# Attention constants dealt out again, rotary finishing steps at other key tiles, first transfers in another order, in a one-core encoder layer on Trainium2

## The chip, the cores and the metric

One core of a Trainium2 chip runs the whole layer. The metric is the device time of one execution in microseconds (us). The engines are TensorE (PE, with its weight loads PEld), VectorE (DVE), ScalarE (ACT), GpSimd (POOL) and SyncE (SP, which issues most transfers).

## What is computed

A hybrid encoder layer on x of 1024 positions by 1024, all in float32:

```
h = rms_norm(x, norm1_g);  z = h @ w_in            # 1024 x 2304: qA kA vA qB kB vB
A: q, k = rope(rms_norm(q)), rope(rms_norm(k))     # 8 q heads, 2 kv heads, 2-D axial rotary
   o_A = softmax(q k^T / 8) v                      # dense, over all 1024 keys
B: three dilated windows with ALiBi, merged by their softmax denominators
x1 = x + concat(norm(o_A), norm(o_B)) @ w_out
y  = x1 + (gelu(gate) * val) @ w_down              # gate, val: conv of rms_norm(x1) @ w_up
```

## The kernel before

The program is written as one Python function that emits instructions; a scheduler sets the final order on each engine, so the order shown below is that of the compiled program. PE runs every large product in three passes of high and low parts (lines such as L279 to L281 and L405 to L407), and the input, up and down projections as seven products in place of eight.

**Start, 0 to 57 us.** SP loads the identity (`ident`, L518), the first tile of x in halves (L520), `norm1_g` (L521), then in turn two halves of the k and v columns of w_in (`kv_load`, L264) and further tiles of x. `x_prep` transposes a tile of x on PE (L180) and splits it into a high part by ACT (L228) and a low part by DVE (L229). `kv_split` does the same for the weights, scaled by norm1_g (L268 on ACT, L269 on DVE). `kv_proj(i)` multiplies tile i by those weights (L279 to L281), `x_rest` squares the tile for its norm (L244) and copies the transposed banks (L248), and `kv_out` evacuates the product (L291).

**Input projection, 27 to 208 us.** `in_product` makes 28 products; ACT evacuates them (L420 to L428) and DVE combines them (L417). The next weights are combined by DVE (L378 to L384) and split (L388 ACT, L389 DVE). Beside it keys and queries get their rotary steps: POOL's `turn` (L285, eight instructions), DVE's `norm` (L490), `cos` (L500), `add` (L503). `k_ready` transposes the keys and writes them to `R_K2A` and `R_KHA` (L332, L333). The unused partitions of `R_KHA` are filled with -1 by `fill_k` (L348), other constants by `fill` (L214).

**Attention A, about 211 to 430 us.** Sixteen blocks g of eight key tiles. A key tile is two products of scores (L624, L625), an exp on ACT (L627) and eight products with v (L619). Beside it the next block is prepared: `mx` makes eight products (L597), each with a maximum by DVE (L598) out of one of two banks, and `last` combines them (L601), to be transposed and evacuated (L605). L576 and L577 split the queries, L592 evacuates their transposes, L639 and L640 finish the output of the block before (`o_norm`). Two lists of further work are taken up beside it: `late`, the squares, root (L486, whose Sqrt needs ACT's table changed and changed back) and norms (L490, followed by POOL's L506) of the qB columns; and `fills`, nine constants for attention B. `late_plan` says how many items of `late` follow each key tile.

Attention B, the mixer and both projections of the MLP take the rest, to 1342 us.

```
act(f(slots[kt], 512), bank(st), AF.Exp)
take(prep, plan[kt])
take(late, late_plan[kt])
```

Of the kernel before, what the change touches and what calls it, by code (L numbers as in the profile page):

```python
# [14 lines left out]
AF = mybir.ActivationFunctionType  # L15
OP = mybir.AluOpType
# [3 lines left out]
D = 1024  # L20
# [12 lines left out]
O_IDF = 0  # L33
# [5 lines left out]
O_QAB = 832  # L39
# [5 lines left out]
R_KHA = R_K2A + 2048  # L45
# [12 lines left out]
R_A = {1: 0, 7: 4096, 6: 8192, 4: 12288, 5: 16384, 2: 20480, 3: 24576}  # L58
# [6 lines left out]
F_JNK = O_F + 4096  # L65
F_CST = O_F + 4608
F_KVT = O_F + 5120
F_KSQ = O_F + 4096
F_ROPE = O_F + 8192
# [3 lines left out]
R_QLN = R_XT + 1024  # L73
# [4 lines left out]
R_VB = R_XT + 8192  # L78
R_QLB = (R_XT + 1024, R_XT + 10240)
R_KN = R_XT + 12288  # L80
R_SET = (R_W, R_K2A)
# [42 lines left out]
def tile_encoder_layer(ctx, tc, x, w_in, gains, outg, norm1_g, norm2_g, w_out, w_up, conv_w, conv_b,  # L124
                       w_down, ident, rope, tmx, tbc, cnt, out):
    nc = tc.nc
# [12 lines left out]
    act = nc.scalar.activation  # L139
# [5 lines left out]
    def f(off, n):  # L145
        return bigf[:, off:off + n]

    def r(off, n):
        return bigr[:, off:off + n]

    def rf(off, n):
        return bigr[:, off:off + n].bitcast(F32)
# [8 lines left out]
    def rp(off, *dims):  # L161
        return raw_ap(bigr[:, off:off + 1], dims)
# [19 lines left out]
    def perm_rows(t, b, width):  # L182
        rr, c = divmod(b, 2)
        return bass.AP(tensor=t.tensor, offset=t.offset + (512 * c + rr) * width, ap=[[4 * width, 128], [1, width]])
# [24 lines left out]
    def qab(tt):  # L209
        return O_QAB + 1024 * tt  # L210

    def fill(dst, n, m, c):

        vec.tensor_scalar(dst, f(O_IDF, m)[:, None, :].to_broadcast([128, n, m]), 0.0, c, op0=OP.mult, op1=OP.add)  # L214

# [127 lines left out]

    def fill_k():
        for i in range(4):
            vec.tensor_scalar(r(R_KHA + 512 * i, 512)[64:128], f(F_ROPE, 512)[64:128], 0.0, -1.0,  # L348
                              op0=OP.mult, op1=OP.add)


    def w_buf(c, half):
# [162 lines left out]
            return [square, root, norm, k_out]  # L515
        return [square] + [root] * (late == 3), [norm, gain]

    dma(f(O_IDF, 128), ident)  # L518
    for i in range(2):
        dma(f(qab(0) + 512 * i, 512), perm_rows(x, 0, D)[:, 512 * i:512 * i + 512])  # L520
    dma(f(F_CST, 128)[0:8], norm1_g.rearrange("(k p) -> k p", p=128))  # L521
    for half in range(2):
        kv_load(half)
        dma(f(qab(1 + half), 1024), perm_rows(x, 1 + half, D))
    dma(f(qab(3), 1024), perm_rows(x, 3, D))
    w_load(0, 0)
    vec.tensor_copy(r(R_IDR, 128), f(O_IDF, 128))
    nc.tensor.transpose(bank(7, 8), f(F_CST, 128)[0:8], f(O_IDF, 8)[0:8])
# [51 lines left out]
    def a_prep(g):  # L580
        b, kv = divmod(g, 2)
        q2 = R_Q2A + 512 * (g % 2)
        ql = R_QLA + 512 * (g % 2)

        def nat():
            q_nat(qab(b) + 256 * kv, 64, vec, 4, 512 * kv)

        def first():
            t = next_tr()
            for i in range(4):  # L590
                tr_r(t, i, r(R_QD + 128 * (4 * kv + i), 128))
            act(r(q2, 512), bank(t), AF.Copy)  # L592

        def mx(i):
            for hf in range(2):
                b = hf
                mm(bank(b), r(q2 + 128 * i, 128), r(R_K2A + 1024 * kv + 512 * hf, 512), start=True, stop=True)  # L597
                vec.tensor_reduce(f(SM_MC + 8 * hf + i, 1), bank(b), axis=AX.X, op=OP.max)  # L598

        def last():  # L600
            vec.tensor_tensor(rp(R_QLN + 512 * kv + 64, [128, 4]), f(SM_MC, 4), f(SM_MC + 8, 4), op=OP.max)  # L601
            t = next_tr()
            for i in range(4):
                tr_r(t, i, r(R_QLN + 128 * (4 * kv + i), 128))
            act(r(ql, 512), bank(t), AF.Copy)  # L605

        return [nat, first] + [lambda i=i: mx(i) for i in range(4)] + [last]
# [309 lines left out]
        eng.tensor_tensor(r(o + 512, 512), t_raw(n, i), rf(o, 512), op=OP.subtract)  # L917


    fills = []  # L920
    for c, v in ((64, 1.0), (192, 0.0)):
        for i in range(2):
            fills.append(lambda o=R_VB + 1024 * i + c, v=v: fill(rp(o, [256, 4], [1, 64]), 4, 64, v))
    fills.append(lambda: fill(rp(R_QLB[1] + 64, [128, 8], [1, 64]), 8, 64, 0.0))
    for i in range(4):
        fills.append(lambda o=R_SET[0] + 2048 + 512 * i: vec.tensor_scalar(
            r(o, 512)[64:128], f(O_QAB, 512)[64:128], 0.0, -1.0, op0=OP.mult, op1=OP.add))

    def take(prep, n):
        for _ in range(n):  # L930
            if prep:
                p = prep.pop(0)
                if p:
                    p()

    prep = [lambda: fill(rp(R_QLN + 64, [128, 8], [1, 64]), 8, 64, 0.0)] + a_prep(0)
    for i in range(4):
        kv_proj(i)
        x_rest(i)
# [97 lines left out]
    for g in range(16):  # L1037
        prep = a_prep(g + 1) if g < 15 else [lambda: b_split(0)] + b_prep(0)
        tail = a_main(g, prep, tail, late, (3, 2, 2, 2, 2, 2, 2, 1) if g == 15 else (1, 1, 1, 1, 1, 1, 1, 0),
                      (0, 1, 1, 0, 1, 0, 1, 0) if g < 3 else (0, 0, 1, 0, 1, 0, 1, 0) if g < 7 else (0, 1, 0, 0, 0, 1, 0, 0))  # L1040
        if g == 7:
            dma(f(F_CNT, 384), cnt)
            gp.memset(fp(F_VCN + 64, [66, 8]), 1.0)
            load_vc(0)
        if g == 11:
            load_k(0)
            load_k(1)
        if g == 5:
            v_split(R_VB, F_VBN)
            load_v(1)  # L1050
        take(fills, 1)
    for t in tail:
        t()
    take(prep, 99)
# [401 lines left out]
```

## Time and profile before

| what | value |
|---|---|
| time, median of 3 runs | 1342.73 us (1342.39 to 1345.34) |
| the profiled execution | 1343.92 us, of which the span is 1342.2 us |
| PE busy | 1311.1 us, 98% of the span |
| DVE, ACT, POOL busy | 991.7 us (74%), 674.0 us (50%), 363.4 us (27%) |

The profiled execution is 1.19 us over the median and has 1.7 us around its span. With PE at 98%, the time is that of PE's work plus the stretches in which PE stands still.

### The profile page before, as it was taken

Reading aid. Unit: us, or ns where it says so; the run is one execution under the profiler, and the core shown is the slowest. Engines: PE = TensorE matmul, PEld = TensorE weight load, DVE = VectorE, ACT = ScalarE, POOL = GpSimd, SP = SyncE. Lnnn points to the kernel's source line nnn. Section 1 sums busy time; section 2 is a strip of 40 time slices with the busy share of each in tenths; the row PEclk is TensorE's granted clock in tenths of the full one; section 3 lists DMA queues with packets and bytes.
Section 4 is the critical chain, followed back from the end, with each engine's and each line's share of the span. In section 5 each row is a group of like instructions: output and inputs, shape, how many; then the busy total and the mean of one; then the engine's idle time right before and its main releaser. Section 6 shows DMA issues by size and latency. Waiting matters only on the chain.

```text
span 1342.2 us, 20068 instructions
## 1 busy us (share of the span) xinstructions
PE 1311.1 (98%) x7559; PEld 1134.9 (85%) x7559; DVE 991.7 (74%) x1613; ACT 674.0 (50%) x1057; POOL 363.4 (27%) x274
## 2 busy tenths in 40 slices
PE   8999999999999999999999999999999999999998
PEld 7999989989998888878877788888888888888887
DVE  4987696864545888876579877887787789586664
ACT  7855553644445776764365444444444445244331
POOL 1611123020001222100114565556656651100000
PEclk9999999999999999999999999999999999999999
DMA  7144212000001333252222233232233325897873
GB/s 256 53 123 114 80 39 65 9 9 0 1 1 34 107 105 81 67 166 79 94 87 71 102 110 111 86 102 96 102 115 105 102 101 190 283 311 228 293 223 113
DMA packets 119859, 148.08 MB, mean 110 GB/s; under 512 B 50833, under 2 KB 76881, under 8 KB 119761
## 3 DMA queue, kind: packets, MB, share of 16 engines
q1 hardware_dynamic: 118609, 143.65, 33.3%
q0 software_dynamic: 1152, 3.15, 0.9%
q8 instruction: 59, 0.97, 0.3%
q14 instruction: 39, 0.32, 0.1%
HBM read 112.95 MB, written 33.82 MB: 109 GB/s over the span
## 4 chain that ended last, share of the span: by engine, by line
PE 70%; DVE 16%; ACT 5%; issue 4%; POOL 4%; DMA 1%; SPq 0%; DVEq 0%; ACTq 0%; POOLq 0%
PE ps L619 7%; PE ps L1161 7%; PE ps L1162 7%; PE ps L1163 7%; PE ps L1277 5%; PE ps L1276 5%; PE ps L1278 5%; DVE bigf L1194 4%; PE ps L624 2%; PE ps L597 2%; PE ps L625 2%; POOL bigf L1208 2%; PE ps L862 2%; PE ps L795 2%; PE ps L864 2%
## 5 line engine op out<-in xcount | busy, mean ns | idle before, releaser
L1161 PE MATMUL ps<-bigr 128*128 128x512 f32 x616 | 241.1, 392 | 6.6 <-DVE bigf L1165 6.1
L1162 PE MATMUL ps<-bigr 128*128 128x512 f32 x616 | 239.8, 389 | 0.0
L1163 PE MATMUL ps<-bigr 128*128 128x512 f32 x616 | 239.7, 389 | 0.0
L1144 ACT ACTIVATE bigr<-bigf 128x512 fp32r<-128x512 f32 x154 | 92.8, 624 | 159.2 <-POOL bigf L1136 95.4
L1194 DVE SCALAR_TENSOR_TENSOR bigf<-bigf 128x768 f32<-128x768 f32 (+1 forms) x176 | 146.4, 889 | 26.3 <-ACT bigf L1192 26.3
L619 PEld LDWEIGHTS ps<-bigf 128*128 128x128 f32 x1024 | 139.4, 191 | 10.5
L1161 PEld LDWEIGHTS ps<-bigr 128*128 128x128 f32 x616 | 115.6, 188 | 35.6 <-DVE bigf L1165 9.9
L1145 DVE TENSOR_TENSOR bigr<-bigf,bigr 128x512 fp32r<-128x512 f32 x112 | 116.5, 1057 | 32.6 <-ACT bigr L1144 32.6
L1256 ACT ACTIVATE bigr<-bigf 128x1024 fp32r<-128x1024 f32 x77 | 80.6, 1059 | 119.5 <-PE ps L1278 76.9
L1163 PEld LDWEIGHTS ps<-bigr 128*128 128x128 f32 x616 | 115.6, 188 | 24.2
L1162 PEld LDWEIGHTS ps<-bigr 128*128 128x128 f32 x616 | 115.6, 188 | 23.6
L619 PE MATMUL ps<-bigf 128*128 128x65 f32 x1024 | 134.3, 267 | 0.0
L405 PE MATMUL ps<-bigr 128*128 128x256 f32 x448 | 127.2, 284 | 1.2 <-ACT bigf L291 1.2
L406 PE MATMUL ps<-bigr 128*128 128x256 f32 x448 | 126.8, 283 | 0.0
L407 PE MATMUL ps<-bigr 128*128 128x256 f32 x448 | 126.7, 283 | 0.0
L627 ACT ACTIVATE bigf<-ps 128x512 f32<-128x512 f32 x128 | 75.7, 597 | 93.5 <-PE ps L625 91.1
L1277 PE MATMUL ps<-bigr 128*128 128x512 f32 x308 | 119.9, 389 | 0.0
L1278 PE MATMUL ps<-bigr 128*128 128x512 f32 x308 | 119.8, 389 | 0.0
L1276 PE MATMUL ps<-bigr 128*128 128x512 f32 x308 | 119.8, 389 | 0.0
L1257 DVE TENSOR_TENSOR bigr<-bigf,bigr 128x1024 fp32r<-128x1024 f32 x77 | 93.0, 1221 | 28.7 <-ACT bigr L1256 26.7
L598 DVE TENSOR_REDUCE bigf<-ps 128x1 f32<-128x512 f32 x128 | 86.0, 689 | 23.6 <-PE ps L597 22.2
L1208 POOL TENSOR_TENSOR bigf<-bigf 128x512 f32<-128x512 f32 x44 | 69.1, 1590 | 89.9 <-DVE bigf L1199 65.6
(221 smaller groups left out, 2892.6 us busy)
## 6 DMA issues: line engine op xcount, KB each, us to landing
bigf<-w_down SPq DMA_DIRECT2D x99, 256.0 KB, 4.3
bigf<-w_up SPq DMA_DIRECT2D x44, 512.0 KB, 4.2
bigf<-gscr SPq DMA_DIRECT2D x77, 256.0 KB, 4.1
gscr<-bigf SPq DMA_DIRECT2D x33, 512.0 KB, 2.7
bigf<-w_in SPq DMA_DIRECT2D x8, 1024.0 KB, 5.3
bigf<-x SPq DMA_DIRECT2D x15, 512.0 KB, 6.6
bigf<-tmx SPq DMA_DIRECT2D x8, 672.0 KB, 5.1
bigf<-w_out SPq DMA_DIRECT2D x8, 512.0 KB, 4.0
```

What stands on the lines that cost most here:

```text
L405: mm(o, ah, wh, start=(k == 0 and t % 2 == 0 and n != 2), stop=False, skip_group_check=True)
L406: mm(o, ah, wl, start=False, stop=False, skip_group_check=True)
L407: mm(o, al, wh, start=False, stop=(k == 3), skip_group_check=True)
L619: mm(bank(ob, 65, 66 * i), f(slots[kt] + 128 * i, 128), f(F_VA + 132 * kt + 66 * kv, 65), start=(kt == 0 and i == 0), stop=(kt == 7), skip ...
L1145: (gp if n in (2, 4) and m > 3 else vec).tensor_tensor(rp(o + 512, [128, 4], [1, 128]), src, rfp(o, [128, 4], [1, 128]), op=OP.subtract)
L1161: mm(bank(b), wh, th, start=(k == 0 and n in (1, 5, 6, 7)), stop=False, skip_group_check=True)
L1162: mm(bank(b), wh, tl, start=False, stop=False, skip_group_check=True)
L1163: mm(bank(b), wl, th, start=False, stop=(k == 3), skip_group_check=True)
L1194: vec.scalar_tensor_tensor(f(a + o, n), f(i + d, n), w_, f(a + o, n), op0=OP.mult, op1=OP.add)
L1276: mm(o, ah, r(d, 512), start=(q == 0 and n in (1, 5, 2)), stop=False, skip_group_check=True)
L1277: mm(o, ah, r(d + 1024, 512), start=False, stop=False, skip_group_check=True)
L1278: mm(o, al, r(d, 512), start=False, stop=(q == NQ - 1), skip_group_check=True)
```

## The change

- `ident` and `norm1_g` are fetched by ACT's queue, ahead of its other work. SP's queue starts with the halves of x's first tile, then both halves of the k and v weights, and only then the other tiles of x.
- A one-element copy on DVE, out of the split weights into the scratch that `x_rest` writes its squares to, is put ahead of the loop over tiles.
- `fill_k` and the fill of `R_QLN` go from DVE to ACT.
- The nine `fills` are taken in blocks 4 to 12, one each, and read the output of the block before.
- `late_plan` has other numbers.

```
...
-    dma(f(O_IDF, 128), ident)
+    nc.scalar.dma_start(f(O_IDF, 128), ident)
+    nc.scalar.dma_start(f(F_CST, 128)[0:8], norm1_g.rearrange("(k p) -> k p", p=128))
     for i in range(2):
         dma(f(qab(0) + 512 * i, 512), perm_rows(x, 0, D)[:, 512 * i:512 * i + 512])
-    dma(f(F_CST, 128)[0:8], norm1_g.rearrange("(k p) -> k p", p=128))
     for half in range(2):
         kv_load(half)
-        dma(f(qab(1 + half), 1024), perm_rows(x, 1 + half, D))
-    dma(f(qab(3), 1024), perm_rows(x, 3, D))
+    for i in range(1, 4):
+        dma(f(qab(i), 1024), perm_rows(x, i, D))
...
-    def fill(dst, n, m, c):
+    def fill(dst, n, m, c, src=O_IDF, eng=None):
+        src = f(src, m)[:, None, :].to_broadcast([128, n, m])
+        if eng is None:
+            vec.tensor_scalar(dst, src, 0.0, c, op0=OP.mult, op1=OP.add)
+        else:
+            act(dst, src, AF.Copy, scale=0.0, bias=c)
...
-            vec.tensor_scalar(r(R_KHA + 512 * i, 512)[64:128], f(F_ROPE, 512)[64:128], 0.0, -1.0,
+            act(r(R_KHA + 512 * i, 512)[64:128], f(F_ROPE, 512)[64:128], AF.Copy, scale=0.0, bias=-1.0)
...
+    vec.tensor_copy(f(F_JNK, 1), rf(R_A[7] + 256, 1))
     for i in range(4):
         kv_proj(i)
         x_rest(i)
...
-                      (0, 1, 1, 0, 1, 0, 1, 0) if g < 3 else (0, 0, 1, 0, 1, 0, 1, 0) if g < 7 else (0, 1, 0, 0, 0, 1, 0, 0))
+                      (1, 1, 0, 0, 0, 0, 1, 1) if g < 3 else (0, 1, 0, 0, 0, 0, 1, 1) if g < 7 else (0, 1, 0, 0, 0, 0, 1, 0))
...
-        take(fills, 1)
+        if g > 3 and fills:
+            fills.pop(0)(qab((g - 1) // 2) + 256 * ((g - 1) % 2))
```

In the order of the compiled program the lines of the changed kernel have other numbers: L228 is L232 there, L244 L248, L248 L252, L268 L272, L291 L295; behind L340 three to seven are added (L382 is L385, L389 L392, L490 L493, L500 L503, L503 L506, L577 L580, L598 L601, L601 L604, L639 L642, L640 L643).

The first place is the start on ACT. Before, from its first row on:

```order
L228 ACT_TABLE_LOAD
L228 ACTIVATE bigr<-ps 128x512 x2
L268 ACTIVATE bigr<-bigf 128x256 x4
L244 ACTIVATE bigf<-bigf 128x1024
L228 ACTIVATE bigr<-ps 128x512
L268 ACTIVATE bigr<-bigf 128x256 x4
L228 ACTIVATE bigr<-ps 128x512
L248 ACTIVATE bigf<-ps 128x512 x2
L291 ACTIVATE bigf<-ps 128x256
```

The same place on ACT in the changed kernel:

```order
L521 DMA bigf<-ident 128x128
L522 DMA bigf<-norm_g 8x128
L232 ACT_TABLE_LOAD
L232 ACTIVATE bigr<-ps 128x512 x2
L272 ACTIVATE bigr<-bigf 128x256 x8
L232 ACTIVATE bigr<-ps 128x512 x2
L295 ACTIVATE bigf<-ps 128x256
L248 ACTIVATE bigf<-bigf 128x1024
L252 ACTIVATE bigf<-ps 128x512 x2
```

The eight weight splits now stand together, and the square and the two copies of tile 0 stand behind the first evacuation of a k and v product instead of ahead of it. On PE the 24 products of `kv_proj(0)` now stand without products of `kv_proj(1)` between them (before, six stood there), and with the eight transposes of x's second tile, as before.

The second place is DVE in the last products of the input projection, ahead of attention. Before:

```order
L490 TENSOR_TENSOR bigf<-bigf 128x4x256
L192 TENSOR_TENSOR bigf<-bigf 128x16
L214 TENSOR_SCALAR bigr<-bigf 128x8x64
L193 SCALAR_TENSOR_TENSOR bigf<-bigf 128x16
L348 TENSOR_SCALAR bigr<-bigf 64x512
L194 SCALAR_TENSOR_TENSOR bigf<-bigf 128x16
L348 TENSOR_SCALAR bigr<-bigf 64x512
L490 TENSOR_TENSOR bigf<-bigf 128x4x256
L348 TENSOR_SCALAR bigr<-bigf 64x512 x2
L382 TENSOR_TENSOR bigf<-bigf 128x4x256
L500 TENSOR_TENSOR bigf<-bigf 128x4x256
L577 TENSOR_TENSOR bigr<-bigf,bigr 128x4x64
```

The same place on DVE in the changed kernel:

```order
L493 TENSOR_TENSOR bigf<-bigf 128x4x256
L192 TENSOR_TENSOR bigf<-bigf 128x16
L385 TENSOR_TENSOR bigf<-bigf 128x4x256
L193 SCALAR_TENSOR_TENSOR bigf<-bigf 128x16
L503 TENSOR_TENSOR bigf<-bigf 128x4x256
L194 SCALAR_TENSOR_TENSOR bigf<-bigf 128x16
L392 TENSOR_TENSOR bigr<-bigf,bigr 128x1024
L493 TENSOR_TENSOR bigf<-bigf 128x4x256
L506 TENSOR_TENSOR bigf<-bigf 128x4x256
L580 TENSOR_TENSOR bigr<-bigf,bigr 128x4x64
```

The five fills are gone to ACT, and the weight sum (L382 before) now stands right behind L192, which is also what POOL's `turn` waits for; `cos` (L500 before) follows it, and a norm (L490) comes behind the split L389.

The third place is block 3 of attention A and the head of block 4, on DVE. Before:

```order
L191 RECIPROCAL bigf<-bigf 128x64
L598 TENSOR_REDUCE bigf<-ps 128x1 x3
L192 TENSOR_TENSOR bigf<-bigf 128x64
L598 TENSOR_REDUCE bigf<-ps 128x1
L193 SCALAR_TENSOR_TENSOR bigf<-bigf 128x64
L601 TENSOR_TENSOR bigr<-bigf 128x4
L194 SCALAR_TENSOR_TENSOR bigf<-bigf 128x64
L490 TENSOR_TENSOR bigf<-bigf 128x4x256
L577 TENSOR_TENSOR bigr<-bigf,bigr 128x4x64
L490 TENSOR_TENSOR bigf<-bigf 128x4x256 x2
L639 RECIPROCAL bigf<-ps 128x4
L490 TENSOR_TENSOR bigf<-bigf 128x4x256
```

The same place on DVE in the changed kernel:

```order
L493 TENSOR_TENSOR bigf<-bigf 128x4x256
L601 TENSOR_REDUCE bigf<-ps 128x1 x3
L493 TENSOR_TENSOR bigf<-bigf 128x4x256
L604 TENSOR_TENSOR bigr<-bigf 128x4
L493 TENSOR_TENSOR bigf<-bigf 128x4x256
L580 TENSOR_TENSOR bigr<-bigf,bigr 128x4x64
L493 TENSOR_TENSOR bigf<-bigf 128x4x256
L601 TENSOR_REDUCE bigf<-ps 128x1 x2
L642 RECIPROCAL bigf<-ps 128x4
```

The four norms now stand apart: one ahead of the last three maxima of block 3, one behind them, the others around L577. On ACT, the Sqrt with its two table loads stood in the middle of block 3's exps; in the changed kernel it stands here, behind the last evacuation for block 3 (L608 there is L605) and ahead of block 3's first exp (L630 there is L627):

```order
L630 ACTIVATE bigf<-ps 128x512
L595 ACTIVATE bigr<-ps 128x512
L608 ACTIVATE bigr<-ps 128x512
L489 ACT_TABLE_LOAD
L489 ACTIVATE bigf<-bigf 128x64
L630 ACT_TABLE_LOAD
L630 ACTIVATE bigf<-ps 128x512 x2
```

On PE, five of block 3's products for maxima (L597) now stand ahead of the first product that has to wait for one of its exps; before, two of them stood there. From block 5 on PE's order is that of before.

## Rows read from the trace of the kernel before

**Rows 1.** Waits of PE: line, releaser: us in total, times, longest us.

```profile
PE ps L597 <- DVE bigf L598: 2.1, 3, 1.1
PE ps L177 <- ACT bigr L333: 1.7, 1, 1.7
PE ps L405 <- ACT bigf L291: 1.2, 2, 0.6
PE ps L597 <- DVE bigf L417: 0.9, 1, 0.9
```

**Rows 2.** Timeline of PE: start, us, line, shapes, idle before and releaser.

```profile
8.63 0.58 PE L279 MATMUL ps<-bigr 128*128 128x256 f32 x1 [2.09 <-ACT bigr L268]
...
12.09 0.41 PE L279 MATMUL ps<-bigr 128*128 128x256 f32 x1
12.30 0.41 PE L280 MATMUL ps<-bigr 128*128 128x256 f32 x1
...
257.69 0.62 PE L597 MATMUL ps<-bigr 128*128 128x512 f32 x2
```

**Rows 3.** Timeline of SP's queue, its first issues.

```profile
0.75 0.38 SPq L518 DMA_DIRECT2D bigf<-ident  x1
1.18 0.90 SPq L520 DMA_DIRECT2D bigf<-x  x2
...
2.54 0.40 SPq L264 DMA_DIRECT2D bigf<-w_in  x1
```

**Rows 4.** Timeline of ACT, 0 to 58 us.

```profile
9.68 1.04 ACT L244 ACTIVATE bigf<-bigf 128x1024 bf16<-128x1024 f32 x1
...
13.26 1.07 ACT L248 ACTIVATE bigf<-ps 128x512 f32<-128x512 f32 x2
16.04 0.39 ACT L291 ACTIVATE bigf<-ps 128x256 f32<-128x256 f32 x1 [1.71 <-PE ps L281]
...
54.29 1.03 ACT L424 ACTIVATE bigf<-ps 128x1024 f32<-128x1024 f32 x1 [0.80 <-DVE bigr L229]
55.21 1.66 ACT L228 ACTIVATE bigr<-bigf 128x512 fp32r<-128x512 f32 x3
```

**Rows 5.** Timeline of DVE, last products of the input projection.

```profile
184.91 1.39 DVE L382 TENSOR_TENSOR bigf<-bigf 128x1024 f32<-128x1024 f32 x1
...
188.83 1.21 DVE L503 TENSOR_TENSOR bigf<-bigf 128x1024 f32<-128x1024 f32 x1
...
197.28 1.22 DVE L417 TENSOR_TENSOR bigf<-ps,bigf 128x1024 f32<-128x1024 f32 x1
```

**Rows 6.** Timeline of POOL: a turn by itself, and three gains in attention block 4.

```profile
214.47 3.38 POOL L285 TENSOR_TENSOR bigf<-bigf 128x128 f32<-128x128 f32 x8 [3.73 <-DVE bigf L417]
...
268.18 8.93 POOL L506 TENSOR_TENSOR bigf<-bigf 128x1024 f32<-128x1024 f32 x3 [1.16 <-DVE bigf L490]
```

**Rows 7.** Timeline of ACT, last products of the input projection.

```profile
187.37 1.00 ACT L424 ACTIVATE bigf<-ps 128x1024 f32<-128x1024 f32 x1
...
188.74 0.58 ACT L333 ACTIVATE bigr<-ps 64x512 fp32r<-64x512 f32 x1
```

**Rows 8.** Timeline of DVE, attention blocks 3 and 4.

```profile
263.22 1.23 DVE L490 TENSOR_TENSOR bigf<-bigf 128x1024 f32<-128x1024 f32 x1
...
264.70 4.53 DVE L490 TENSOR_TENSOR bigf<-bigf 128x1024 f32<-128x1024 f32 x2
...
269.25 3.29 DVE L490 TENSOR_TENSOR bigf<-bigf 128x1024 f32<-128x1024 f32 x1
```

**Rows 9.** Timeline of ACT, attention block 3.

```profile
257.21 1.28 ACT L486 ACT_TABLE_LOAD   x1
258.50 0.26 ACT L486 ACTIVATE bigf<-bigf 128x64 f32<-128x64 f32 x1
```

**Rows 10.** Groups of DVE by line, whole span: busy us, mean ns, idle before.

```profile
L598 DVE TENSOR_REDUCE bigf<-ps 128x1 f32<-128x512 f32 x128 | 86.0, 689 | 23.6 <-PE ps L597 22.2
...
L214 DVE TENSOR_SCALAR bigr<-bigf 128x256 fp32r<-128x256 f32 (+1 forms) x6 | 1.6, 324 | 0.0
```

More of the change, by code (lines that the diff above doesn't have):

```diff
@@ L210, in qab @@
         return O_QAB + 1024 * tt
-    def fill(dst, n, m, c):
-        vec.tensor_scalar(dst, f(O_IDF, m)[:, None, :].to_broadcast([128, n, m]), 0.0, c, op0=OP.mult, op1=OP.add)
+    def fill(dst, n, m, c, src=O_IDF, eng=None):
[4 more added lines that the diff above has]
+            act(dst, src, AF.Copy, scale=0.0, bias=c)
     INW = 2304
@@ L347, in fill_k @@
         for i in range(4):
-            vec.tensor_scalar(r(R_KHA + 512 * i, 512)[64:128], f(F_ROPE, 512)[64:128], 0.0, -1.0,
-                              op0=OP.mult, op1=OP.add)
+            act(r(R_KHA + 512 * i, 512)[64:128], f(F_ROPE, 512)[64:128], AF.Copy, scale=0.0, bias=-1.0)
     def w_buf(c, half):
@@ L922, in tile_encoder_layer @@
         for i in range(2):
-            fills.append(lambda o=R_VB + 1024 * i + c, v=v: fill(rp(o, [256, 4], [1, 64]), 4, 64, v))
-    fills.append(lambda: fill(rp(R_QLB[1] + 64, [128, 8], [1, 64]), 8, 64, 0.0))
+            fills.append(lambda g, o=R_VB + 1024 * i + c, v=v: fill(rp(o, [256, 4], [1, 64]), 4, 64, v, g))
+    fills.append(lambda g: fill(rp(R_QLB[1] + 64, [128, 8], [1, 64]), 8, 64, 0.0, g))
     for i in range(4):
-        fills.append(lambda o=R_SET[0] + 2048 + 512 * i: vec.tensor_scalar(
-            r(o, 512)[64:128], f(O_QAB, 512)[64:128], 0.0, -1.0, op0=OP.mult, op1=OP.add))
+        fills.append(lambda g, o=R_SET[0] + 2048 + 512 * i: vec.tensor_scalar(
+            r(o, 512)[64:128], f(g, 64)[64:128][:, None, :].to_broadcast([64, 8, 64]), 0.0, -1.0,
+            op0=OP.mult, op1=OP.add))
     def take(prep, n):
@@ L934, in take @@
                     p()
-    prep = [lambda: fill(rp(R_QLN + 64, [128, 8], [1, 64]), 8, 64, 0.0)] + a_prep(0)
+    prep = [lambda: fill(rp(R_QLN + 64, [128, 8], [1, 64]), 8, 64, 0.0, eng=act)] + a_prep(0)
+    vec.tensor_copy(f(F_JNK, 1), rf(R_A[7] + 256, 1))
     for i in range(4):
```

## The prediction

> **What bounds the kernel now.** PE is busy for 98% of the span, so a change that leaves PE's work alone can only move the stretches in which PE stands still. I therefore read PE's table of waits first. Of its entries, those that this change can reach are four [rows 1]: 2.1 us in three places where a product for maxima waits for a bank that DVE's maximum (L598) frees, 1.7 us once for the last evacuation of keys (L333), 1.2 us in two places for L291, the longest 0.6, and 0.9 us once for a combination of DVE (L417). Then I went through the timelines of the engines named there: ACT over the start, DVE, ACT and POOL over the last products of the input projection, and DVE, POOL and ACT in blocks 3 and 4 of attention. At each place the question is which chain ends last there in the new order. Everything behind block 5 has PE's old order, and a PE that waits for nothing new; I take it at nothing.
>
> **The start.** SP issues the first half of the k and v weights at 2.54. In the new order only the two halves of x stand ahead of it; the first issue of the queue is at 0.75, those halves take 0.90, so it leaves at 1.65, 0.89 earlier [rows 3]. PE's first product with those weights, at 8.63 after 2.09 us of waiting [rows 2], can follow: 7.74. From there to the end of the first k and v product PE now has 24 products and 8 transposes; at the pitch of 0.21 that rows 12.09 and 12.30 show [rows 2], that is 6.7 us, so about 14.4. Before, that end let L291 start at 16.04 [rows 4]. This is the gain, and the price stands on ACT: the square (1.04) and the two copies (1.07), which ran in the shadow of PE before, now stand behind L291 (0.39), so ACT is through at 14.4 + 0.39 + 1.04 + 1.07 = 16.9, against 16.43 before [rows 4]. ACT has hardly an idle moment in the stretch behind it, so it carries 0.4 of it on. At 54.29 ACT waits 0.80 for DVE ahead of L424, and three L228 of 0.55 each follow it [rows 4] before the L291 that PE waits 0.6 for [rows 1]. In the new order two of those L228 stand ahead of L424 and fill that 0.80. So L291 comes 0.8 - 0.4 = 0.4 earlier, and PE gains 0.4. Bounds: if the first product starts 0.89 earlier and nothing is late, PE gains that and the 0.6, together 1.5; if the weights land no sooner and the end stays at 16.0, ACT is 2.1 late. Moving the two small transfers to ACT's queue costs nothing, since ACT has nothing to do until x has been transposed; without that cover it would be two issues, 0.38 each by SP's row [rows 3].
>
> **The last products of the input projection.** DVE loses a fill (one of a group of six, 0.32 on average [rows 10]) and four L348, and the weight sum L382 moves from 184.91 [rows 5] to right behind L192, about 179.9. POOL's turn, released by the same L192, takes 3.38 by itself [rows 6]; behind the sum (about 1.2, the length of L490 at 263.22 [rows 8], the same shape) it ends near 184.5. ACT's L388 then lies beside the turn; L424 (1.00), L332 and L333 (0.58 each) follow [rows 7], and the keys are there at 186.7 instead of 189.32. PE had been there since 189.32 - 1.7 = 187.6, so its wait of 1.7 [rows 1] goes whole. But it does not stay gained. On DVE, behind the turn, stand cos, a split, the moved norm and L503, four of about 1.2: the last ends at 189.4, before at 190.04 [rows 5]. From there the old chain runs: a split and evacuations on ACT, a table load, L388, L389, L417, whose end at 198.50 [rows 5] released PE. So the product that waits 0.9 for it moves by 0.6 if all of that is one chain, and by 1.7 + 0.9 = 2.6 if none of it binds. I take 0.9, near the chain, because part of the evacuations hang on PE and not on L503. The fills put on ACT cost nothing: ACT is idle for several us ahead of its L388 there; uncovered they would be five of about 0.6.
>
> **Block 3.** A table load takes 1.28, the Sqrt 0.26, and the instruction behind a load starts 0.01 after it [rows 9]. The two loads and the Sqrt, 2.8 in all, now stand ahead of the first exp, on which PE's scores hang. PE covers part with five products for maxima. These have two banks, so the third waits for the first maximum and the fifth for the third: three maxima of 0.69 [rows 10] and an o_norm between them, about 2.5, in which PE has five products of 0.23 (two take 0.62 with their tail [rows 2]) and four transposes. It stands still for about 1.4. Bounds 0 and 2.8; the row of the maxima is the nearest, so 1.4 lost.
>
> The Trainium skill (ScalarE: Activation LUTs, What ACT_TABLE_LOAD costs) puts a switch of tables at 2.66 us, a load of 1.28 and a drain of 1.38. The trace agrees with the load and shows no drain beside it. By the page's figure the term would be an estimated 2.8 worse.
>
> **Block 4.** An L490 by itself takes 1.23 (263.22). Beside POOL's L506 the one at 269.25 takes 3.29, and two take 4.53 [rows 8], while three L506 with one norm between them take 8.93 [rows 6]: one engine stands still for the length of the other's instruction. That is what makes block 4's maximum late, and PE waits 1.1 [rows 1]. In the new order the first L506 lies beside three maxima, which read other memory. But L577 stands between the third and the fourth norm. It hangs on PE's transposes, so POOL's second L506 should have started before it; when that ends, L577 runs, POOL's third L506 already waits, and the fourth norm comes behind it. From the end of L577 to the first maximum's end that is an L506, a norm and 0.69, 4.0 in all, just what the blocked norm of before and its maximum took (3.29 + 0.69) when PE waited 1.1. On top comes the time that L577 itself waits for the second L506: PE's transposes fall into that instruction's last third, 0.7 of its 2.1 (3.29 less 1.23). I take 0.7 lost. If DVE goes first each time, the whole 1.1 is gained; if POOL gains one more instruction on it, 2.1 is lost.
>
> The Trainium skill (SBUF — State Buffer, Who interferes with whom) says that a DVE instruction with two SBUF inputs and a GpSimd instruction that reads SBUF exclude each other, and that order of issue decides who blocks. The trace agrees, with 3.29 against 1.23. A rule by which both merely slowed down would give the 1.1 back.
>
> **Blocks 1, 2 and 5 to 15.** The order around the two shorter waits on L598 stays. The nine fills, 0.3 to 0.4 each, go where DVE waits 22.2 us for PE over 128 maxima [rows 10]; without that cover they would be 3.4 together.
>
> **The sum.** 0.4 + 0.9 - 1.4 - 0.7 = -0.8: the profiled execution of 1343.92 would become 1344.7. It is 1.19 above the median of the runs, so I forecast a median of 1343.5, no measurable change; 0.2%, or 2.7 us, is about what a measurement here can tell.
>
> **The rivals.** *Clean gain, faster.* PE's waits go and nothing takes their place: 0.6 at the start, 2.6 in the projection, nothing lost in block 3, 1.1 in block 4, together 4.3: 1338.4. For it: each wait is on the list, and each of the edits touches its releaser. Against it: L417's wait hangs on a chain that hardly moves, and the table loads are in the way. 33 in 100.
>
> *Late ACT, slower.* The weights' second half, or x behind it, lands no sooner, the first k and v product ends near 16.0, and ACT's 2.5 us (0.39, 1.04, 1.07 [rows 4]) behind it make everything 2.1 late, which the 0.80 no longer covers as DVE is late too: -2.1 + 0.9 - 1.4 - 0.7 = -3.3, so 1346.0. It decides from an end at about 15.4 on. For it: the splits wait for both halves now. Against: 0.89 of earlier issue. 15 in 100.
>
> *Dear tables, slower.* If a switch held ACT longer than load and Sqrt, by some 2.8, PE would lose that more: 1346.3. The page on ScalarE would have it so; row 258.50 with its 0.01 speaks against it. 5 in 100.
>
> *Nothing happens*, the projection's gain given back whole at L417 and the blocks' stalls only moved, lies within the forecast: 1342 to 1343. With it the forecast has 47 in 100, its own range 1341.0 to 1345.0.
>
> **Numbers.** Faster 0.33, same 0.47, slower 0.20. The range takes in the clean gain's time and most of the late ACT: 1338.4 to 1345.8.
>
> **What would show it.** The first L279 near 7.7 and L291 near 14.4; ACT's idle time ahead of L424 gone; no wait on L333, but one on L417 near 198; a gap of 1 to 2 us in PE at the head of block 3, where two table loads stand; in block 4 an L490 of over 3 us and a wait on L598. I am wrong if PE meets its maxima in both blocks without waiting, or if the k and v product ends after 15.4.

## The result, and the profile after

The changed kernel takes 1346.73 us, median of 20 runs (1345.22 to 1348.53); the kernel before, in 20 runs, 1343.93 (1342.36 to 1346.10). The ratio is 1.0019, interval 1.0013 to 1.0025: it is slower, by 2.6 us (0.0019 of 1344). The forecast was 1343.5, no measurable change, in a range that ends at 1345.8.

The profiled execution is the 1348.53, the longest of the 20, with a span of 1346.8; the one of before was 1343.92, at its median. First the waits of PE that answer to [rows 1] (line, releaser, total, times, longest):

```profile
PE ps L600 <- DVE bigf L601: 3.0, 5, 1.3
PE ps L408 <- ACT bigf L295: 2.7, 1, 2.7
PE ps L600 <- ACT bigr L670: 1.7, 1, 1.7
```

The wait for the keys (L333, now L337) is gone. One of 1.7 stands ahead of attention; the wait on L295 (L291 before) grew from 1.2 in two places to 2.7 in one, that on the maxima from 2.1 to 3.0. How much later the same product of PE starts than before says what each place cost: 0.1 at 30 us, 0.5 at 46, 3.3 at 62, 1.4 at 195, 2.2 at 201, 3.5 at 270, 4.1 at 300, 4.6 at the end. So in this execution the start loses 3.3, 2.7 of it between 46 and 62 us, the projection gives back 1.1, block 3 loses 1.3 and block 4 0.6.

**Start.** DVE, then POOL, then ACT, then PE, with start, duration, line, shapes, idle time and releaser:

```profile
45.26 0.14 DVE L249 TENSOR_SCALAR bigf<-bigf 128x1 f32<-128x1 f32 x1
45.32 2.33 DVE L973 TENSOR_SCALAR bigf<-bigf 128x8 f32<-128x8 f32 x1
47.56 2.39 DVE L392 TENSOR_TENSOR bigr<-bigf,bigr 128x1024 fp32r<-128x1024 f32 x1
49.87 1.79 DVE L233 TENSOR_TENSOR bigr<-bigf,bigr 128x512 fp32r<-128x512 f32 x1
...
52.18 0.68 DVE L256 TENSOR_TENSOR bigf<-ps,bigf 128x512 f32<-128x512 f32 x1
...
45.20 2.42 POOL L385 TENSOR_TENSOR bigf<-bigf 128x1024 f32<-128x1024 f32 x1
47.57 1.30 POOL L257 TENSOR_TENSOR bigf<-bigf 128x512 f32<-128x512 f32 x1
48.95 2.17 POOL L258 TENSOR_TENSOR bigf<-bigf 128x512 f32<-128x512 f32 x1
...
52.90 0.63 ACT L232 ACTIVATE bigr<-bigf 128x512 fp32r<-128x512 f32 x1 [2.41 <-DVE bigf L256]
54.62 1.15 ACT L232 ACTIVATE bigr<-bigf 128x512 fp32r<-128x512 f32 x2 [1.09 <-POOL bigf L257]
55.67 0.36 ACT L295 ACTIVATE bigf<-ps 128x256 f32<-128x256 f32 x1
...
56.09 0.38 PE L408 MATMUL ps<-bigr 128*128 128x256 f32 x1 [2.67 <-ACT bigf L295]
...
58.51 0.42 PE L408 MATMUL ps<-bigr 128*128 128x256 f32 x1
58.72 0.41 PE L409 MATMUL ps<-bigr 128*128 128x256 f32 x1
...
59.96 0.28 PE L409 MATMUL ps<-bigr 128*128 128x256 f32 x1
60.08 0.28 PE L410 MATMUL ps<-bigr 128*128 128x256 f32 x1
```

A DVE instruction on eight numbers a partition takes 2.33 and ends as POOL's weight sum does, which began 0.12 ahead of it; the split behind it takes 2.39, beside POOL's next copy. In the kernel before these two take 0.15 and 1.21. They start there when POOL's sum is done (43.73 and 2.41 make 46.14) or about to be, and the split is 0.08 ahead of POOL's next copy. DVE, ACT and PE before:

```profile
46.08 0.15 DVE L966 TENSOR_SCALAR bigf<-bigf 128x8 f32<-128x8 f32 x1
46.15 1.21 DVE L389 TENSOR_TENSOR bigr<-bigf,bigr 128x1024 fp32r<-128x1024 f32 x1
...
49.60 0.68 DVE L252 TENSOR_TENSOR bigf<-ps,bigf 128x512 f32<-128x512 f32 x1
...
53.12 0.37 ACT L291 ACTIVATE bigf<-ps 128x256 f32<-128x256 f32 x1
...
53.54 0.39 PE L405 MATMUL ps<-bigr 128*128 128x256 f32 x1 [0.65 <-ACT bigf L291]
```

The 128x8 instruction and the split together last 3.4 longer in the changed kernel. DVE had been 0.8 ahead, so its L256 starts at 52.18, 2.6 later than before (L252, 49.60); L232 waits 2.41 for it, and L295 starts at 55.67 where it was at 53.12. Behind its wait PE then issues products 0.21 apart, 0.12 from 60 us on: the clock granted to TensorE is 0.58 of its full rate between 56 and 59 us, so most of that stretch is at the lower of its two levels (1.2 and 2.4 GHz), called the half clock below. The wait costs 2.0 more than the one of before, the half clock 1.5.

**Blocks 3 and 4.** ACT, PE, DVE, POOL:

```profile
256.92 1.28 ACT L630 ACT_TABLE_LOAD   x1
258.21 1.08 ACT L630 ACTIVATE bigf<-ps 128x512 f32<-128x512 f32 x2
...
258.27 1.10 PE L600 MATMUL ps<-bigr 128*128 128x512 f32 x2 [0.25 <-DVE bigf L601]
259.79 0.50 PE L600 MATMUL ps<-bigr 128*128 128x512 f32 x1 [0.43 <-DVE bigf L601]
275.75 1.11 PE L600 MATMUL ps<-bigr 128*128 128x512 f32 x2 [1.28 <-DVE bigf L601]
...
269.90 1.87 DVE L580 TENSOR_TENSOR bigr<-bigf,bigr 128x256 fp32r<-128x256 f32 x1 [0.64 <-PE ps L177]
271.69 3.40 DVE L493 TENSOR_TENSOR bigf<-bigf 128x1024 f32<-128x1024 f32 x1
...
268.12 5.89 POOL L509 TENSOR_TENSOR bigf<-bigf 128x1024 f32<-128x1024 f32 x2 [2.16 <-DVE bigr L604]
```

This is the forecast picture: two table loads ahead of the first exp, PE held by the two banks for maxima; then L580 (L577 before) behind POOL's second gain and the last norm behind the third, 3.40 here and 3.29 in [rows 8].

### The profile page after: what moved, and what is told of

Its sections match the earlier page's. It is cut to its first block, busy times and chain, and to the rows that moved or that the text cites. A ratio compares the mean times of both kernels' runs of the same rounds, so it can differ in the third digit from the quotient of the medians.

```text
span 1346.8 us, 20070 instructions
## 1 busy us (share of the span) xinstructions
PE 1314.3 (98%) x7559; PEld 1135.8 (84%) x7559; DVE 989.7 (73%) x1609; ACT 677.4 (50%) x1062; POOL 361.8 (27%) x274
## 4 chain that ended last, share of the span: by engine, by line
PE 78%; DVE 11%; ACT 4%; issue 3%; POOL 2%; DMA 2%; SPq 0%; ACTq 0%; DVEq 0%; POOLq 0%
PE ps L1169 9%; PE ps L1170 9%; PE ps L1171 9%; PE ps L622 7%; PE ps L1285 5%; PE ps L1286 5%; PE ps L1284 5%; PE ps L627 2%; PE ps L600 2%; PE ps L628 2%; PE ps L798 2%; PE ps L865 2%; PE ps L867 2%; PE ps L866 2%; PE ps L793 2%
## 5 line engine op out<-in xcount | busy, mean ns | idle before, releaser
L630 ACT ACTIVATE bigf<-ps 128x512 f32<-128x512 f32 x128 | 75.8, 596 | 95.7 <-PE ps L628 94.7
L601 DVE TENSOR_REDUCE bigf<-ps 128x1 f32<-128x512 f32 x128 | 86.1, 689 | 20.6 <-PE ps L600 19.0
```

## The experiments

Each kernel ran in batches with the kernel before; medians of before were 1343.9 to 1344.4. "Slower by" is from the ratio, whose interval stands beside it.

### Each part alone

The new start alone, transfers and copy, and then its transfers without the copy (the last line below):

```
-    dma(f(O_IDF, 128), ident)
+    nc.scalar.dma_start(f(O_IDF, 128), ident)
+    nc.scalar.dma_start(f(F_CST, 128)[0:8], norm1_g.rearrange("(k p) -> k p", p=128))
...
+    vec.tensor_copy(f(F_JNK, 1), rf(R_A[7] + 256, 1))
```

> The kernel before with the new order of the first transfers and the one-element copy, nothing else. Theory 1 (the start costs it: VectorE and GpSimd meet on the same memory port at 45 to 52 us, ScalarE's L291 comes late and TensorE stands still near 53 us): 2.0 to 3.3 us slower than before, 1345.9 to 1347.2 beside a before of 1343.9, with a wait of 2 to 3 us for L291. Theory 2 (the prediction's sum: the start gains 0.4 and something behind it costs more than forecast): 0.4 us faster to even.

> The kernel before with the new order of the first transfers only, without the one-element copy. If the transfers' order is what makes VectorE and GpSimd meet: slower by 2 us or more, as with the whole start. If the copy is, which holds ScalarE's square of the first tile back behind the weight splits: even with before, or up to 0.9 us faster, as the weights come 0.9 earlier.

1344.22, ratio 1.0003 (0.9994 to 1.0012), and 1344.65, 1.0005 (0.9996 to 1.0014). The copy changes nothing in the time that can be measured. The start alone is no gain, but not the loss of 2 that was expected either, and PE waits 1.5 for L291 once where before it waited 1.2 in two places. DVE's 128x8 instruction takes 2.31 here too, but the split behind it gets ahead of POOL:

```profile
46.18 2.31 DVE L967 TENSOR_SCALAR bigf<-bigf 128x8 f32<-128x8 f32 x1
48.40 1.21 DVE L389 TENSOR_TENSOR bigr<-bigf,bigr 128x1024 fp32r<-128x1024 f32 x1
...
48.42 2.35 POOL L253 TENSOR_TENSOR bigf<-bigf 128x512 f32<-128x512 f32 x1
```

They start 0.02 apart; in the changed kernel, with 0.01 between them, the split took 2.39 and POOL's copy 1.30. Up to 100 us the order of the instructions on every engine is the same in the two kernels, so one order gives waits of 1.5 or of 2.7.

The constants of attention A on ACT, without the rest:

```
-            vec.tensor_scalar(r(R_KHA + 512 * i, 512)[64:128], f(F_ROPE, 512)[64:128], 0.0, -1.0,
-                              op0=OP.mult, op1=OP.add)
+            act(r(R_KHA + 512 * i, 512)[64:128], f(F_ROPE, 512)[64:128], AF.Copy, scale=0.0, bias=-1.0)
...
-    prep = [lambda: fill(rp(R_QLN + 64, [128, 8], [1, 64]), 8, 64, 0.0)] + a_prep(0)
+    prep = [lambda: fill(rp(R_QLN + 64, [128, 8], [1, 64]), 8, 64, 0.0, eng=act)] + a_prep(0)
```

> The kernel before with fill_k and the fill of R_QLN on ScalarE, nothing else. Theory 1: the wait of 1.7 us for L333 goes, the one for L417 grows to about 1.7, 1.1 us faster than before (1342.8 beside 1343.9). Theory 2, by which moved constants cost time: even or slower.

1344.61, 1.0004 (0.9995 to 1.0013): no gain alone. First its timelines of PE and DVE, then its windows behind that wait (length, busy us of PE, PEld, DVE, ACT and POOL, granted clock, DMA share, GB/s):

```profile
198.63 1.19 PE L600 MATMUL ps<-bigr 128*128 128x512 f32 x2 [2.47 <-DVE bigf L420]
...
195.00 1.22 DVE L216 TENSOR_SCALAR bigr<-bigf 128x256 fp32r<-128x256 f32 x5
```

```profile
198.00:201.00 3.00, 2.37 (x9) 2.21 (x9) 2.96 (x3) 0.24 (x1) 1.29 (x1) 0.52 0.86 285
201.00:204.00 3.00, 2.98 (x12) 2.49 (x12) 2.12 (x4) 0.00 (x0) 0.00 (x0) 0.50 0.84 261
```

The wait for keys is gone, 1.9 won, but the gain of 1.1 that was expected does not come. Five fills of attention B, which stand there in the kernel before too, take 1.2 of DVE just ahead of L392 and L420; the end of L420 (L417 before) moves by nothing (198.49, before 198.50), and PE's wait there grows from 0.9 to 2.5, which takes the 1.9 back. Behind it the clock is 0.5 for two windows, 1.2 lost by 201 us and 2.2 by 210. In the changed kernel these five, taken later and bound, are out of the way. That pairing the forecast did not see: it costed each edit by itself.

The nine bound fills alone:

```
-        take(fills, 1)
+        if g > 3 and fills:
+            fills.pop(0)(qab((g - 1) // 2) + 256 * ((g - 1) % 2))
```

> The kernel before with the nine constants of attention B taken in blocks 4 to 12 behind the output of the block before, nothing else; its order in blocks 3 and 4 is that of the changed kernel. Theory 1: two table loads at the head of block 3 and the norms of block 4 behind GpSimd cost 1.8 us (1345.7 beside 1343.9), with three short waits at the head of block 3 and one of 1.3 in block 4. Theory 2, by which that order gives its waits back: even.

1346.74, 1.0024 (1.0015 to 1.0033): 3.2 slower, the whole loss of the change and more. Its waits on maxima are 2.7 in four places, the longest 1.3 as in the changed kernel, and the order of blocks 3 and 4 shown ahead of the prediction is this kernel's too. This kernel has the old numbers of `late_plan`, and its trace has the changed kernel's order on DVE and POOL all through attention A; so the new numbers have no part in it. It is the fills, taken later and bound to an output, that move the norms, the Sqrt and the gains; taking them later and binding them were not tried apart.

### Undoing the start

The changed kernel with the transfers of before and without the copy:

> The changed kernel with the first transfers and the copy as before, so constants on ScalarE and bound constants together. Theory 1 (the parts act together: with the fills gone from VectorE, the chain behind L417 ends 1.1 us earlier, and blocks 3 and 4 lose 1.9): 0.8 to 2.2 us slower than before, 1344.7 to 1346.1. Theory 2 (the parts add up: 0.6 for the constants alone and 3.0 for the bound constants alone, in the means): 3.6 slower, 1347.5.

1345.83, 1.0013 (1.0004 to 1.0022). So beside the rest the start costs 0.8 by the ratios, give or take about 1.5, so it may be nothing; it is not the 3.3 of the one profiled execution. And the windows of its block 4, behind a wait of 1.28 at 272.82 that is the changed kernel's at 275.75 (PE's line first, then windows as above):

```profile
272.82 1.09 PE L600 MATMUL ps<-bigr 128*128 128x512 f32 x2 [1.28 <-DVE bigf L601]
...
273.00:276.00 3.00, 2.90 (x14) 2.36 (x14) 2.08 (x5) 0.00 (x0) 1.60 (x1) 0.72 0.38 87
276.00:279.00 3.00, 3.00 (x13) 2.71 (x12) 1.09 (x2) 0.60 (x1) 0.00 (x0) 0.50 0.00 0
279.00:282.00 3.00, 3.00 (x14) 2.68 (x14) 1.30 (x3) 0.60 (x1) 0.00 (x0) 0.64 0.00 0
```

The changed kernel's windows there show 1.00:

```profile
276.00:279.00 3.00, 2.90 (x20) 2.45 (x20) 2.27 (x6) 0.60 (x1) 1.53 (x1) 1.00 0.38 87
279.00:282.00 3.00, 3.00 (x22) 2.70 (x21) 2.36 (x4) 0.63 (x2) 0.00 (x0) 1.00 0.00 0
```

The same order, the same wait, and block 4 costs 3.7 in one execution and 0.6 in the other. The 11 runs of this kernel spread from 1344.05 (mean granted clock 0.999) to 1348.40 (0.996).

### What holds the blocks: the gains

The late gains (L506) go from POOL to DVE, in the kernel with the bound fills alone, in the changed kernel, and in the changed kernel without its start:

```
-            gp.tensor_tensor(q3, q3, fp(O_GB, [0, 4], [0, 4], [1, 64]), op=OP.mult)
+            (gp if late is None else vec).tensor_tensor(q3, q3, fp(O_GB, [0, 4], [0, 4], [1, 64]), op=OP.mult)
```

> The bound constants as in bound_alone, with the four gains (L506) behind the late norms on VectorE instead of GpSimd. If GpSimd's hold on the memory port is what makes block 4 wait 1.4 us: no norm takes over 1.3 us, the wait at the head of block 4 falls to at most 0.7, and the kernel is about 1 us faster than bound_alone, 1345.7; the waits at the head of block 3 stay. If VectorE's sheer amount of work is it: even with bound_alone or slower, since VectorE gets four instructions of 1.2 us more.

> The changed kernel with the four gains of the late norms on VectorE instead of GpSimd, nothing else. If block 4's collision and the half clock behind it are most of what the change costs: 2.5 to 3 us faster than the changed kernel, 1343.8 to 1344.2, even with before. If block 4 only adds to costs that lie elsewhere (start, projection): at most 1 us faster than the changed kernel, 1345.7.

> The same without the new start: constants on ScalarE, bound constants, late gains on VectorE. By the parts measured so far (1.1 gained ahead of attention, less what the half clock takes back there; 1.3 lost at the head of block 3; the 1.3 that before waits in block 4 gained, and 0.4 more): 0.5 to 1.5 us faster than before, 1342.5 to 1343.5, and 0.6 faster than after_gain. If the start costs nothing: even with after_gain.

1344.13, 0.9998 (0.9990 to 1.0007); 1344.51, 1.0002 (0.9993 to 1.0011); 1343.77, 0.9997 (0.9988 to 1.0006). Against the same kernel with the gains on POOL that is 3.5, 2.3 and 2.2 less by the ratios, give or take about 1.6 each; the first is far more than the 1 that was expected. DVE has more work, and PE waits less. DVE in block 4 of the first of the three:

```profile
267.57 0.43 DVE L581 TENSOR_TENSOR bigr<-bigf,bigr 128x256 fp32r<-128x256 f32 x1 [0.63 <-PE ps L177]
...
270.13 1.39 DVE L602 TENSOR_REDUCE bigf<-ps 128x1 f32<-128x512 f32 x2 [1.00 <-PE ps L601]
...
271.52 1.20 DVE L494 TENSOR_TENSOR bigf<-bigf 128x1024 f32<-128x1024 f32 x1
```

The query split takes 0.43 in place of 1.87 and the norm 1.20 in place of 3.40, so the meetings of norm and gain are gone, and with them the loss. But the last norm also stands behind block 4's first maxima now, where it stood ahead of them: the edit takes away the meeting and a place in the order at once, and no run says how much each is worth. Block 3 still loses 1.3 behind its table loads here, and by the end of block 6 PE has won 1.5 back.

### What stands ahead of attention

The first five fills on ACT, unbound; then with the gains on DVE as well; and the constants on ACT with 16 products that no one reads put ahead of the first product for maxima (added work; nothing is left out):

```
-            fills.append(lambda o=R_VB + 1024 * i + c, v=v: fill(rp(o, [256, 4], [1, 64]), 4, 64, v))
+            fills.append(lambda o=R_VB + 1024 * i + c, v=v: fill(rp(o, [256, 4], [1, 64]), 4, 64, v, eng=act))
...
+            if g == 0:
+                t = next_tr()
+                for i in range(16):
+                    mm(bank(t, 256), r(R_QD + 512 * kv, 128), r(R_A[1], 256), start=True, stop=True)
```

> The kernel before with fill_k, the fill of R_QLN and the first five of the nine constants on ScalarE, the other four where they were; its order in blocks 3 and 4 is that of before. If the five fills ahead of the split L389 are what kept the constants alone from gaining: the wait for L417 falls from 2.5 to about 1.4 us, and the kernel is 1.1 us faster than before, 1342.8. If that chain hangs on ScalarE or GpSimd instead: as with the constants alone, even with before to 0.6 slower.

> five_act with the late gains on VectorE: before's order up to the middle of block 3, so no table loads at the head of block 3. If the waits read in the traces are all there is: 0.9 gained ahead of attention and 1.3 in block 4, 1.5 to 2.2 us faster than before, 1341.8 to 1342.5. If VectorE has no room for four instructions of 1.2 us in blocks 3 to 5: even with five_act, 1343.5.

> The constants on ScalarE as in consts_alone, and 16 products without a reader (128x256, about 1.9 us) on TensorE straight ahead of the product that waits 2.5 us for L417. They only add work. If a long wait is what lets the granted clock fall to half behind it: no half clock at 198 to 205 us, and 0.6 to 0.8 us faster than consts_alone in the mean, about even with before. If the clock falls for another reason: even with consts_alone, or slower by the part of 1.9 us that does not fit into the wait.

1343.48, 0.9997 (0.9988 to 1.0006); 1343.61, 0.9991 (0.9982 to 1.0000); 1344.80, 1.0007 (0.9999 to 1.0016). The fills on ACT delay the evacuations there: PE waits 2.2 for L595 instead. The first does not gain the 1.1 that was expected; the second gains 1.2 of the 1.5 to 2.2, at the edge of its interval. The added products keep the clock at 1.00 over 186 to 230 us, yet the kernel is no faster than without them: they take 2.2 themselves, so this tells nothing of the clock's price.

With those five fills on ACT, but in blocks 8 to 12, bound to the output of the block before, the other four as before in time, and the gains on DVE; and with 12 such products:

```
+        if 4 < g < 9:
+            take(fills, 1)
+        if g > 7 and fills5:
+            fills5.pop(0)(qab((g - 1) // 2) + 256 * ((g - 1) % 2))
```

> five_gain with the five constants taken later, in blocks 8 to 12 on ScalarE, bound behind the block before, so that they stand ahead of nothing in front of attention. In five_gain TensorE waited 2.1 us for L592 (L595 there), which stood behind those five. If that is so: the wait falls by about 1 us, to 1.1, and the kernel is 1 us faster than five_gain and 1.5 to 2.5 faster than before, 1341.8 to 1342.7. If L417 or another link ends as late: even with five_gain, 1343.5.

> late_gain with 12 products without a reader (128x256, about 1.4 us) on TensorE ahead of the product that waits. If standing still is what lets the clock fall: no half clock in front of attention, more executions at a mean clock of 0.999, and even with late_gain to 1 us faster, though there is 1.4 us more work. If not: the clock falls as in late_gain and the kernel is even to 1 us slower. A small part of attention B's order differs between the two, by which they may be 0.5 us apart either way.

1342.80, 0.9996 (0.9987 to 1.0005), and 1343.01, 0.9996 (0.9988 to 1.0005): as before, within the interval. In the first of them the Sqrt is where it was before, in the middle of block 3's exps, and the last two norms stand behind block 4's maxima. A wait of 1.8 on L670 is left ahead of attention in the first; the second trades it for the products.

### What holds the start: the weight sum

The three early weight sums (L380, L382 and L384 before, 2.4 to 2.7 each on POOL) go from POOL to DVE: with the new start alone, in the kernel before, and in the changed kernel together with the gains.

```
-        eng = vec if c else gp
+        eng = vec
```

> start_alone with the first three weight sums (L382 and its like, 2.4 us each on GpSimd) on VectorE. If meeting on the memory port is what makes L291 late: no VectorE instruction of over 2 us at 44 to 50 us, the wait of 1.5 us or more for L291 falls to at most 0.7, and the kernel is 0.5 to 1 us faster than start_alone, 1343.5. If it is the late square and copies on ScalarE: the wait stays at 1.5 or more.

> The kernel before with one edit: the two early weight sums that stood on POOL stand on DVE; start and all else as before. Theory A (the gain of start_sums comes from taking the sum out of DVE's way under the new transfer order): without the new order there is little to win, since before's L966 and L389 missed POOL's sum anyway: within 0.5 of 1344. Theory B (sums on DVE are better by themselves, whatever the start): 1342.6, as start_sums.

> The changed kernel with both suspects taken out: the early weight sums on DVE and the four late gains on DVE. If the meetings of POOL and DVE at the two places are what the change lost, their removals add up: after 1346.7, less 2.2 for the gains (after_gain) and 1.7 for the sums (start_sums against start_alone) gives 1342.8, below before. If the start's loss has another cause in this kernel: 1344.5, as after_gain.

1342.57, 0.9992 (0.9983 to 1.0001); 1343.95, 0.9996 (0.9987 to 1.0005); 1342.02, 0.9983 (0.9974 to 0.9992). The new start improves by 1.5 with it, the start of before by 0.5, both within what the intervals allow to be nothing. In the changed kernel it is worth 2.6 (from 1.0002, with the gains on DVE already), give or take about 1.7, and both moves together 4.8: from measurably slower to measurably faster. The start on DVE in that last kernel, and two of PE's waits in it:

```profile
45.00 1.21 DVE L385 TENSOR_TENSOR bigf<-bigf 128x1024 f32<-128x1024 f32 x1
46.13 1.78 DVE L233 TENSOR_TENSOR bigr<-bigf,bigr 128x512 fp32r<-128x512 f32 x1
...
49.03 1.21 DVE L392 TENSOR_TENSOR bigr<-bigf,bigr 128x1024 fp32r<-128x1024 f32 x1
```

```profile
PE ps L600 <- DVE bigf L601: 1.7, 4, 0.8
PE ps L600 <- ACT bigr L670: 1.6, 1, 1.6
```

Sum and split take 1.21 each, the wait on L295 has left the list, and PE is 1.4 ahead of before at 62 us. DVE's order is another too: L233 is now ahead of L392.

The traces say more than the times here, since this stretch can be read by itself: the ten other kernels with the start of before agree with it there within 0.04. Between 46 and 62 us, against the kernel before, PE loses 2.7 in the changed kernel, 0.1 in the new start alone, 0.2 with its transfers alone and 0.1 in the changed kernel with the gains on DVE; it wins 1.6 in each of the three kernels with the new start and the sums on DVE (the third is the last one below), and 0.3 with the sums on DVE and the start of before. The changed kernel with the gains on DVE has the changed kernel's order on every engine up to 100 us. DVE, POOL and PE in it:

```profile
45.34 2.31 DVE L973 TENSOR_SCALAR bigf<-bigf 128x8 f32<-128x8 f32 x1
47.56 1.21 DVE L392 TENSOR_TENSOR bigr<-bigf,bigr 128x1024 fp32r<-128x1024 f32 x1
...
47.58 2.35 POOL L257 TENSOR_TENSOR bigf<-bigf 128x512 f32<-128x512 f32 x1
...
54.94 0.38 PE L408 MATMUL ps<-bigr 128*128 128x256 f32 x1 [1.50 <-ACT bigf L295]
```

Here DVE's split, 0.02 ahead of POOL's copy, took 1.21; PE's wait is 1.50, and the clock stays at 1.00 behind it. So which of the two is held at 47.6 us makes 1.2 of PE's wait, in one and the same order, and the half clock came behind the longer wait only.

The version that the runs point to is `late_gain` with the new start and these sums on DVE:

> The best of both: late_gain (1342.80) with the new start and the early weight sums on DVE (start_sums, 1342.57; each 1.1 to 1.4 below before). If the gains add: 1341.4. If the start's gain is eaten by the next waits: 1342.8.

1341.49, 0.9977 (0.9967 to 0.9987): 3.1 faster than before, and the time that was expected if the gains add. Its interval and that of the changed kernel with both moves overlap, so which of the two is better stays open.

## Why the prediction was wrong

Two steps failed, the base from which the time was counted and the gain at the start; and the sum has no term for the half clock.

**The base.** "It is 1.19 above the median of the runs": the median of three runs was taken for the kernel's, and 1.19 taken off. Over 20 runs the median is 1343.93, and the profiled 1343.92 was typical. This put the forecast 1.2 low; with the sum's own 1344.7 it would have been 2.0 low in place of 3.2. So the base failed too, and the times of the range are 1.2 lower by it.

**The start, the step that failed.** The first L283 starts at 7.81 (7.7 forecast), L295 at 14.11 (14.4), ACT is through its copies at 16.65 (16.9), and its idle 0.80 ahead of L424 is gone. The sentence that failed is the next one, "L291 comes 0.8 - 0.4 = 0.4 earlier". It looks at the L291 behind L424 (56.77 before), and PE's wait came at the one ahead of it, which starts 2.6 later (53.12 before, 55.67 now). I followed ACT's queue to 57 us and took DVE's and POOL's for unchanged. Behind POOL's weight sum and copies DVE came 2.6 late, and ACT waited for it elsewhere. The rule that I used for block 4, a norm takes 3.29 beside a gain, was not asked of the start, though POOL's 2.41 for the sum stands in the trace of before at 43.73. Nor did PE keep its early lead: the first product is 0.8 earlier, but at 30 us PE is 0.1 behind the kernel before.

Against 0.4 gained in the forecast, the start cost 0.4 alone and 0.8 beside the rest by the ratios, and either may be nothing. What is clear is that the gain is missing, and the traces say where: 0.1 lost between 46 and 62 us in two executions and 2.7 in the third, 1.6 won in three where POOL does not have the sum. That DVE's meeting with POOL makes L295 late is shown by the two executions of one order with waits of 2.67 and 1.50. That the rest of the 1.6 is the same meeting, and not DVE's other order once it has the sums, is argued.

**The projection** came out near in number, 0.9 forecast and 1.1 in the profile, with the wait for the keys gone and one of 1.7 at 200.82. DVE, ACT and PE:

```profile
199.45 1.22 DVE L420 TENSOR_TENSOR bigf<-ps,bigf 128x1024 f32<-128x1024 f32 x1
...
200.13 0.62 ACT L670 ACTIVATE bigr<-bigf 128x512 fp32r<-128x512 f32 x1
...
200.82 0.70 PE L600 MATMUL ps<-bigr 128*128 128x512 f32 x2 [1.67 <-ACT bigr L670]
```

The trace names L670 on ACT for it, whose end at 200.75 lies 0.08 behind that of L420 (L417 before); either would hold PE. But the nearness is luck. The forecast drew the 0.9 from the constants, and `consts_alone` shows that they move L420 by nothing; the 1.1 came once the five fills had left DVE, which the forecast did not count there. In two other executions with this order (`after_gain`, `undone_gain`) the half clock stands behind that wait (0.60 and 0.50 in windows of 3 us), and PE loses 0.5 and 0.1 there in place of winning 1.1. By the ratios the constants are worth 1.5 beside the bound fills (1.0024 less 1.0013), and cost 0.5 without them, each give or take more than 1.

**Block 3** was right: 1.4 forecast, 1.3 measured, and the exp starts 0.01 behind its load. The rival of dear tables is out, and with it the drain of 1.38 that the Trainium skill (ScalarE: Activation LUTs, What ACT_TABLE_LOAD costs) adds to a load: the exp at 258.21 follows a load of 1.28 that began at 256.92.

**Block 4**: the mechanism was right to the instruction, with the norm at 3.40 and L580 held by the second gain, though for 1.4 and not 0.7; PE lost 0.6 in the profile, 0.7 in the forecast. Together with block 3 the forecast was 2.1 lost. In the traces of the changed kernel and of the bound fills alone, at full clock there, the two blocks cost 1.9 each; in `start_undone`, with the half clock, 5.1. The forecast has no term for the half clock. By the ratio the bound fills alone cost 3.2 (2.0 to 4.4), so 2.1 is just inside. The mean granted clock of their ten runs is 0.9966 on average, that of the runs of before beside them 0.9980; 0.0014 of 1345 us is an estimated 1.9 lost to the half clock, enough for the 1.1 between. Where it came in those runs is not shown: in the profiled one it stands around 193 us, behind a wait of 1.9 for the keys, and not in block 4.

**Sum.** By the ratios the parts, a gain with a plus, are -0.8 for the start (1.0019 less 1.0013), +1.5 for the projection and -3.2 for the blocks. They are differences along one row of kernels and add up to the 2.6 that was lost whatever the truth of each; only the last is clear of zero. Forecast: +0.4, +0.9, -2.1. So two terms of three look too good, by 1.2 and 1.1, and the third gave back 0.6. The traces of single executions are finer; here the other way round, how much later (+) or earlier (-) PE gets in each stretch, against the kernel before:

| kernel | start, 46 to 62 us | projection, 180 to 206 us | blocks 3 and 4, by 420 us |
|---|---|---|---|
| forecast | -0.4 | -0.9 | +2.1 |
| changed kernel | +2.7 | -1.1 | +1.9 |
| `after_gain` | +0.1 | +0.5 | 0.0 |
| `start_undone` | 0.0 | -1.1 | +5.1 |
| `bound_alone` | 0.0 | +0.3 | +1.9 |
| `after_both` | -1.6 | -1.1 | 0.0 |

The rival "dear tables" gave the nearest time, 1346.3, and "late ACT" the next, 1346.0, but neither gave the cause: the exp follows its load by 0.01, and the first k and v product, which was to end near 16.0, ended in time.

## What to carry to other kernels

Where a queue's order changes, lay DVE and POOL side by side over the whole stretch, not only at the place that one is looking at: an instruction of 0.15 lasted 2.33 there, and moving POOL's sums and gains to DVE won 4.8, where the new order had lost 2.6. Edits that fill the same stretch are costed together, since one may only push the other's work onto the critical chain. And a profile is one execution: take the base from many runs, and give a single wait of PE a range that has the half clock behind it in.

## What the runs showed of the hardware

- A DVE operation on 128x8 with one input took 0.15 or, begun 0.12 to 0.13 behind POOL's sum, 2.31 to 2.33 (three executions). The same operation on 128x1 took 0.14 within the same sum (45.26). The Trainium skill (SBUF — State Buffer, Who interferes with whom) lets tensor_scalar take the pair of ports shared with GpSimd in its two-port modes; the trace agrees, with 2.33 for an instruction that ends within 0.03 of POOL's 2.42.
- A DVE and a POOL instruction that came 0.01 to 0.02 apart, in one order of the program, took 1.21 and 2.35 in two executions (47.56 and 48.40) and 2.39 and 1.30 in a third (47.56).
- Behind a wait of 1.28 the granted clock was 1.00 in one execution, and 0.72, 0.50 and 0.64 over 273 to 282 us in another of the same order there (0.50 is 1.2 GHz in place of 2.4). PE was idle for the same time ahead of both, so a trace of one execution does not tell what such a wait costs.
